# Storing the last sums of a row-sum kernel: 128 neighbouring rows, a transpose on VectorE and a last store of four pieces

## Chip, cores, metric

One core of a Trainium2 chip. The metric is the device time of one execution in microseconds (us); medians of several runs are quoted. "Issue" below is the instruction by which SyncE or ScalarE starts a transfer (a DMA), and "landing" the last of the counts on a semaphore by which the transfer tells that it is done. A "piece" is one stretch of bytes from one partition. "Tail" means the stretch from the landing of the last load to the end of the profiled span. All runs with more than one execution are fast, with a granted clock of 1.0.

## The reference

```python
batch, seq, dim = 32, 512, 1024
x = np.random.randn(batch, seq, dim).astype(np.float32)

def reference(x):
    return np.sum(x, axis=-1).astype(np.float32)
```

16,384 rows of 1024 fp32 numbers, 67.1 MB in all, each reduced to one number; the output is 64 KB.

## The kernel before

Rows are dealt out in eight groups. In each group partition p holds 16 neighbouring rows (64 KB of one piece of memory), so its 16 sums are also neighbours in the output: 64 B. Seven groups are loaded and summed mostly on VectorE; ScalarE takes half of the seventh. The eighth is cut into smaller and smaller loads (8, 5, 2 rows, then the last row in two pieces of 560 and 464 columns), so that little work is left after the last byte has landed.

```python
x_g = x.flatten_outer_dims().rearrange("(g p j) d -> g p j d", p=P, j=BIG)     # BIG = 16
out_v = out.rearrange("b s -> (b s)").rearrange("(g p j) -> p g j", p=P, j=BIG)
# ... seven groups, then of the eighth:
rows(t, 0, 8, j, 4)
rows(t, 8, 5, j + 8, 2, pairs=True)
two = rows(t, 13, 2, j + 13, 1, pairs=True)
# ...
nc.sync.dma_start(out=part, in_=rows_from(j, 1)[:, 0, :c])
nc.sync.dma_start(out=whole[:, 1 : width + 1], in_=rows_from(j, 1)[:, 0, c:])
hold(store(nc.scalar, 0, last), two, "its packets come behind those of the loads")
halves(whole[:, :1], part)               # sum of the first 560 columns
halves(sums[:, j : j + 1], whole)        # that sum and the other 464 columns
store(nc.sync, last, last + 1)           # 128 partitions, 64 B each
```

`halves` adds the two halves of a row and accumulates them in one VectorE instruction, followed by a read of the accumulator. A helper moves the wait for the last store to the instruction that clears the semaphores at the very end; all other semaphores are waited for earlier, on SyncE, ahead of two rounds of barriers.

Of the kernel before, what the change touches and what calls it, by code (L numbers as in the profile page):

```python
# [100 lines left out]
@with_exitstack  # L101
def kernel(
    ctx: ExitStack,
    tc: tile.TileContext,
    x: bass.AP,
    out: bass.AP,
):
    nc = tc.nc
    nc.at_finalize(issue_first_load_at_entry)
    nc.at_finalize(order_waits)  # L110
    nc.at_finalize(wait_for_the_store_at_the_clear)
    fp32 = mybir.dt.float32
    P = 128
    batch, seq, dim = x.shape
    rows = batch * seq
    J = rows // P
    BIG = 16


    x_g = x.flatten_outer_dims().rearrange("(g p j) d -> g p j d", p=P, j=BIG)  # L120
    out_v = out.rearrange("b s -> (b s)").rearrange("(g p j) -> p g j", p=P, j=BIG)

    def rows_from(j, n):
        return x_g[j // BIG, :, j % BIG : j % BIG + n, :]



    last = J // BIG - 1
    FIRST = 4
    pieces = (560, 464)  # L130

    with (
        tc.tile_pool(name="in", bufs=3) as inpool,
        tc.tile_pool(name="unread", bufs=4, space=bass.MemoryType.PSUM) as upool,
        tc.tile_pool(name="stage", bufs=1) as stpool,
        tc.manual_schedule(),
    ):
        sums = stpool.tile([P, J], fp32)

        def vec(dst, src):  # L140
            return nc.vector.tensor_reduce(  # L141
                out=dst, in_=src, axis=mybir.AxisListType.X, op=mybir.AluOpType.add
            )

        def hold(inst, until, reason):
            tc.add_manual_dep(
                inst.ins,
                until.ins.name,
                mybir.DependencyInfo(mybir.DependencyClass.Sync, mybir.DependencyReason.DATA),
                reason=reason,  # L150
            )

        def halves(dst, src):
            n = src.shape[-1] // 2
            return nc.vector.tensor_tensor_reduce(  # L155
                out=src[:, :n],
                in0=src[:, :n],
                in1=src[:, n:],
                scale=1.0,
                scalar=0.0,  # L160
                op0=mybir.AluOpType.add,
                op1=mybir.AluOpType.add,
                accum_out=dst,
            )

        def act(dst, src, n):
            unread = upool.tile([P, dim], fp32)
            nc.scalar.activation(  # L168
                out=unread[:, :n],
                in_=src,  # L170
                func=mybir.ActivationFunctionType.Copy,
                accum_out=dst,
            )

        sums_of = []

        def rows(t, a, n, j, n_act, pairs=False):
            nv = n - n_act
            block = t[:, a * dim : (a + n) * dim].rearrange("p (n d) -> p n d", d=dim)
            load = nc.sync.dma_start(out=block, in_=rows_from(j, n))  # L180
            if pairs:
                for q in range(nv):
                    sums_of.append(halves(sums[:, j + q : j + q + 1], block[:, q, :]))
            else:
                sums_of.append(vec(sums[:, j : j + nv], block[:, :nv, :]))
            for q in range(nv, n):
                act(sums[:, j + q : j + q + 1], block[:, q, :], dim)
            return load

        def store(eng, g0, g1):  # L190
            return eng.dma_start(
                out=out_v[:, g0:g1],
                in_=sums[:, g0 * BIG : g1 * BIG].rearrange("p (g j) -> p g j", j=BIG),
            )

        for g in range(last):
            t = inpool.tile([P, BIG * dim + 4], fp32)
            if g == 0:
                rows(t, 0, FIRST, 0, 0)
                first = sums_of[-1]  # L200
                rows(t, FIRST, BIG - FIRST, FIRST, 0)
                continue
            load = rows(t, 0, BIG, g * BIG, BIG // 2 if g == last - 1 else 0)
            if g == 1:
                hold(load, first, "no descriptors of later loads while the first ones start")

        t = inpool.tile([P, BIG * dim + 4], fp32)
        j = last * BIG
        rows(t, 0, 8, j, 4)
        rows(t, 8, 5, j + 8, 2, pairs=True)  # L210
        two = rows(t, 13, 2, j + 13, 1, pairs=True)
        a = BIG - 1



        j += a
        c, width = pieces
        whole = t[:, a * dim + c : BIG * dim + 2]
        nc.vector.memset(whole[:, width + 1 :], 0.0)  # L219
        part = t[:, a * dim : a * dim + c]  # L220
        nc.sync.dma_start(out=part, in_=rows_from(j, 1)[:, 0, :c])  # L221
        nc.sync.dma_start(out=whole[:, 1 : width + 1], in_=rows_from(j, 1)[:, 0, c:])
        hold(store(nc.scalar, 0, last), two, "its packets come behind those of the loads")
        halves(whole[:, :1], part)
        halves(sums[:, j : j + 1], whole)
        store(nc.sync, last, last + 1)


# [28 lines left out]
```

## Time and profile before

| | before |
|---|---|
| median of the first 3 runs | 162.08 us (161.59 to 162.23) |
| span of the profiled execution | 159.6 us |
| queue of loads | 97.8% of the 16 engines' span |
| VectorE, ScalarE busy | 75%, 11% |
| tail, from the last load's landing (157.43) | 2.2 us |

How to read it: an engine at 75% is not the bound where a queue of loads is at 97.8%; a change that keeps the bytes of the loads can act on the tail, or on the pace of the last loads. The lines are shown and read in the prediction. The page and its views round to 0.01 us or 0.1 us; where three decimals stand below, they are from the trace's own records of instructions, packets and semaphore counts.

### The profile page before, as it was taken

How to read it: one execution, taken by the hardware profiler on the slowest of the kernel's cores; microseconds unless marked ns; L12 is line 12 of the kernel's file. 1: busy time of each engine (PE TensorE's matmuls, PEld its weight loads, DVE VectorE, ACT ScalarE, POOL GpSimd, SP SyncE). 2: the span in 40 equal slices, each digit the busy share in tenths (PEclk: the TensorE clock that was granted, in tenths of full speed). 3: DMA queues.
4: the chain of work that ended last, by engine and by line, in shares of the span. 5: the costliest groups of instructions: out<-in, count | busy, mean ns of one | idle time of the engine just before them, and what ended most of it. 6: DMA issues, size and time to landing. Idle time of an engine off the chain costs nothing.

```text
span 159.6 us, 125 instructions
## 1 busy us (share of the span) xinstructions
DVE 120.1 (75%) x22; ACT 17.3 (11%) x31; POOL 0.2 (0%) x4
## 2 busy tenths in 40 slices
DVE  0290059960799958999499994999949999497953
ACT  3000000000000000000000000000000000496953
POOL 0000000000000000000000000000000000000000
DMA  7999996996996989979969969969969969798984
GB/s 263 460 406 579 394 526 263 526 526 263 526 526 263 526 378 411 526 312 476 526 279 509 526 263 526 526 263 526 526 263 526 509 279 526 337 452 371 467 365 128
DMA packets 2928, 67.18 MB, mean 421 GB/s; under 512 B 1264, under 2 KB 1392, under 8 KB 1520
## 3 DMA queue, kind: packets, MB, share of 16 engines
q1 hardware_dynamic: 2016, 67.12, 97.8%
q10 hardware_dynamic: 912, 0.06, 0.4%
HBM read 67.11 MB, written 0.07 MB: 421 GB/s over the span
## 4 chain that ended last, share of the span: by engine, by line
DMA 73%; DVE 25%; SPq 1%; issue 0%; DVEq 0%
DMA t<-in_x_dram 73%; DVE sums L141 24%; SPq L180 1%; SPq L221 0%; DVE t L155 0%; DVEq L252 0%
## 5 line engine op out<-in xcount | busy, mean ns | idle before, releaser
L141 DVE TENSOR_REDUCE sums<-t 128x16 f32<-128x16384 f32 (+3 forms) x9 | 116.6, 12954 | 35.3 <-DMA t<-in_x_dram 35.3
L168 ACT ACTIVATE unread<-t 128x1024 f32<-128x1024 f32 x15 | 15.2, 1012 | 139.2 <-DMA t<-in_x_dram 139.2
L155 DVE CUSTOM_DVE_ANT_0 t<-t 128x512 f32<-128x512 f32 (+2 forms) x6 | 3.5, 602 | 2.4 <-DMA t<-in_x_dram 2.4
L168 ACT ACTIVATION_READ_ACCUMULATOR unread<-t 128x1 f32 x15 | 2.8, 187 | 0.0
L168 ACT ACT_TABLE_LOAD x1 | 1.3, 1283 | 0.8 <-PEq L241 0.8
L155 DVE DVE_READ_ACCUMULATOR2_ANT sums<- 128x1 f32 x5 | 0.4, 83 | 0.0
L241 POOL MEMSET const-uint8-127<- 128x1 uint8 x1 | 0.1, 102 | 0.0
L241 POOL MEMSET const-bfloat16-1.0<- 128x1 bf16 x1 | 0.1, 101 | 0.0
L241 POOL MEMSET const-float32-0.0<- 128x1 f32 x1 | 0.1, 98 | 0.2 <-issue 0.2
L241 POOL MEMSET const-float32-1.0<- 128x1 f32 x1 | 0.1, 98 | 0.0
L155 DVE DVE_READ_ACCUMULATOR2_ANT t<- 128x1 f32 x1 | 0.1, 81 | 0.0
L219 DVE MEMSET t<- 128x1 f32 x1 | 0.1, 59 | 0.0
## 6 DMA issues: line engine op xcount, KB each, us to landing
t<-in_x_dram SPq DMA_DIRECT2D x1, 6144.0 KB, 20.9
t<-in_x_dram SPq DMA_DIRECT2D x1, 4096.0 KB, 31.1
t<-in_x_dram SPq DMA_DIRECT2D x1, 2560.0 KB, 36.9
t<-in_x_dram SPq DMA_DIRECT2D x1, 2048.0 KB, 7.1
t<-in_x_dram SPq DMA_DIRECT2D x1, 1024.0 KB, 38.9
t<-in_x_dram SPq DMA_DIRECT2D x1, 280.0 KB, 39.1
t<-in_x_dram SPq DMA_DIRECT2D x1, 232.0 KB, 39.2
t<-in_x_dram SPq DMA_DIRECT2D x6, 40.8
```

Source lines behind the costliest of these rows:

```text
L141: return nc.vector.tensor_reduce(out=dst, in_=src, axis=mybir.AxisListType.X, op=mybir.AluOpType.add)
L155: return nc.vector.tensor_tensor_reduce(out=src[:, :n], in0=src[:, :n], in1=src[:, n:], scale=1.0, scalar=0.0, op0=mybir.AluOpType.add, op ...
L168: nc.scalar.activation(out=unread[:, :n], in_=src, func=mybir.ActivationFunctionType.Copy, accum_out=dst,)
L180: load = nc.sync.dma_start(out=block, in_=rows_from(j, n))
L219: nc.vector.memset(whole[:, width + 1 :], 0.0)
L241: nc = _bacc.Bacc("TRN2", target_bir_lowering=False, num_devices=1)
```

## The change

The intent: the last store of before writes 8 KB in 128 pieces of 64 B, although only one of 16 sums in each piece is new. If the last row of each partition comes from 128 neighbouring rows, its 128 sums are 512 B in one piece of the output. VectorE turns the column of sums in blocks of 32 by 32, so that four partitions (0, 32, 64, 96) hold 32 sums each, and the last store has 4 pieces of 128 B. The other 15 sums of each partition leave earlier, by a second store on ScalarE's queue. Core of the diff:

```diff
+    SQ = 32
+    REST = BIG - 1
+    x_m = x_r[whole_groups:dense].rearrange("(p j) d -> p j d", j=REST)
+    out_m = out_r[whole_groups:dense].rearrange("(p j) -> p j", j=REST)
+    x_e = x_r[dense:]
+    out_e = out_r[dense:].rearrange("(b q) -> b q", q=SQ)
 ...
+        column = stpool.tile([P, SQ], fp32)
+        turned = stpool.tile([P, SQ], fp32)
+        nc.gpsimd.memset(column, 0.0)
 ...
-        nc.sync.dma_start(out=part, in_=rows_from(j, 1)[:, 0, :c])
-        nc.sync.dma_start(out=whole[:, 1 : width + 1], in_=rows_from(j, 1)[:, 0, c:])
-        hold(store(nc.scalar, 0, last), two, "its packets come behind those of the loads")
+        nc.sync.dma_start(out=part, in_=x_e[:, :c])
+        nc.sync.dma_start(out=whole[:, 1 : width + 1], in_=x_e[:, c:])
+        stored = nc.scalar.dma_start(
+            out=out_g, in_=sums[:, :j].rearrange("p (g j) -> p g j", j=BIG)
+        )
+        hold(stored, two, behind)
+        stored = nc.scalar.dma_start(out=out_m, in_=sums[:, j : j + REST])
+        hold(stored, two, behind)
         halves(whole[:, :1], part)
-        halves(sums[:, j : j + 1], whole)
-        store(nc.sync, last, last + 1)
+        halves(column[:, 0:1], whole)
+        nc.vector.transpose(out=turned, in_=column)
+        nc.sync.dma_start(out=out_e, in_=turned[0:P:SQ, :])
```

More of the change, by code (lines that the diff above doesn't have):

```diff
@@ L114 @@
     batch, seq, dim = x.shape
-    rows = batch * seq
-    J = rows // P
+    rows_total = batch * seq
+    J = rows_total // P
     BIG = 16
-    x_g = x.flatten_outer_dims().rearrange("(g p j) d -> g p j d", p=P, j=BIG)
-    out_v = out.rearrange("b s -> (b s)").rearrange("(g p j) -> p g j", p=P, j=BIG)
+    SQ = 32
+    REST = BIG - 1
+    last = J // BIG - 1
+    x_r = x.flatten_outer_dims()
+    out_r = out.rearrange("b s -> (b s)")
+    whole_groups = last * P * BIG
+    x_g = x_r[:whole_groups].rearrange("(g p j) d -> g p j d", p=P, j=BIG)
+    out_g = out_r[:whole_groups].rearrange("(g p j) -> p g j", p=P, j=BIG)
+    dense = rows_total - P
+    x_m = x_r[whole_groups:dense].rearrange("(p j) d -> p j d", j=REST)
+    out_m = out_r[whole_groups:dense].rearrange("(p j) -> p j", j=REST)
+    x_e = x_r[dense:]
+    out_e = out_r[dense:].rearrange("(b q) -> b q", q=SQ)
     def rows_from(j, n):
-        return x_g[j // BIG, :, j % BIG : j % BIG + n, :]
-    last = J // BIG - 1
+        g, j = divmod(j, BIG)
+        if g < last:
+            return x_g[g, :, j : j + n, :]
+        return x_m[:, j : j + n, :]
     FIRST = 4
@@ L177, in rows @@
         def rows(t, a, n, j, n_act, pairs=False):
+            sums_to = sums[:, j : j + n]
             nv = n - n_act
@@ L182, in rows @@
                 for q in range(nv):
-                    sums_of.append(halves(sums[:, j + q : j + q + 1], block[:, q, :]))
+                    sums_of.append(halves(sums_to[:, q : q + 1], block[:, q, :]))
             else:
-                sums_of.append(vec(sums[:, j : j + nv], block[:, :nv, :]))
+                sums_of.append(vec(sums_to[:, :nv], block[:, :nv, :]))
             for q in range(nv, n):
-                act(sums[:, j + q : j + q + 1], block[:, q, :], dim)
+                act(sums_to[:, q : q + 1], block[:, q, :], dim)
             return load
-        def store(eng, g0, g1):
-            return eng.dma_start(
-                out=out_v[:, g0:g1],
-                in_=sums[:, g0 * BIG : g1 * BIG].rearrange("p (g j) -> p g j", j=BIG),
-            )
         for g in range(last):
@@ L210 @@
         rows(t, 8, 5, j + 8, 2, pairs=True)
+        a = BIG - 1
         two = rows(t, 13, 2, j + 13, 1, pairs=True)
-        a = BIG - 1
-        j += a
         c, width = pieces
@@ L220 @@
         part = t[:, a * dim : a * dim + c]
-        nc.sync.dma_start(out=part, in_=rows_from(j, 1)[:, 0, :c])
-        nc.sync.dma_start(out=whole[:, 1 : width + 1], in_=rows_from(j, 1)[:, 0, c:])
-        hold(store(nc.scalar, 0, last), two, "its packets come behind those of the loads")
+        nc.sync.dma_start(out=part, in_=x_e[:, :c])
+        nc.sync.dma_start(out=whole[:, 1 : width + 1], in_=x_e[:, c:])
+        behind = "its packets come behind those of the loads"
+        stored = nc.scalar.dma_start(
[4 more added lines that the diff above has]
+        hold(stored, two, behind)
         halves(whole[:, :1], part)
-        halves(sums[:, j : j + 1], whole)
-        store(nc.sync, last, last + 1)
+        halves(column[:, 0:1], whole)
+        nc.vector.transpose(out=turned, in_=column)
+        nc.sync.dma_start(out=out_e, in_=turned[0:P:SQ, :])
 _INS = ['x']
```

## The prediction

> **What bounds the kernel now.** I read the page from the top, then the chain of waits in order of time, then the timeline of the last microseconds, because the diff touches only the last group of rows and the end. The page first: engine shares, DMA queues, totals.
>
> ```profile
> span 159.6 us, 125 instructions
> ...
> DVE 120.1 (75%) x22; ACT 17.3 (11%) x31; POOL 0.2 (0%) x4
> ...
> q1 hardware_dynamic: 2016, 67.12, 97.8%
> ...
> HBM read 67.11 MB, written 0.07 MB: 421 GB/s over the span
> ```
>
> The queue of loads keeps the 16 engines busy for 97.8% of the span, VectorE is busy for 75%: the kernel is bound by its loads. The change loads the same bytes, so it can only act after or at the very end of that stream. The chain that ended last, in order of time (start, length, what), says which work that is:
>
> ```profile
> 118.20 39.23 DMA t<-in_x_dram
> 157.43 0.02 issue
> 157.45 0.40 DVE t L155
> 157.85 0.01 DVEq L252
> ```
>
> From 118.20 it is loads without a break. The last one lands at 157.43, then one VectorE sum, and at 157.85 the body is over: 2.2 us of the 159.6 come after the stream. The timeline of those 2.2 us (start, length, engine, line, operation):
>
> ```profile
> 157.06 0.19 ACT L168 ACTIVATION_READ_ACCUMULATOR unread<-t 128x1 f32 x1
> 157.21 0.08 DVE L155 DVE_READ_ACCUMULATOR2_ANT t<- 128x1 f32 x1
> 157.45 0.40 DVE L155 CUSTOM_DVE_ANT_0 t<-t 128x233 f32<-128x233 f32 x1 [0.16 <-DMA t<-in_x_dram]
> 157.78 0.08 DVE L155 DVE_READ_ACCUMULATOR2_ANT sums<- 128x1 f32 x1
> 157.89 0.35 SPq L191 DMA_DIRECT2D out_dram<-sums  x1
> ```
>
> ScalarE has its last sum at 157.25, VectorE at 157.86, and 0.03 us later the last store (8 KB, 128 pieces of 64 B) is issued. The list of DMA issues gives the time to landing of both stores (56 KB of the first seven groups, and the last 8 KB):
>
> ```profile
> out_dram<-sums ACTq DMA_DIRECT2D x1, 56.0 KB, 2.1
> out_dram<-sums SPq DMA_DIRECT2D x1, 8.0 KB, 1.4
> ```
>
> Windows of 0.2 us (DVE, ACT, POOL busy, clock, DMA share, GB/s) cut the last store's 1.4 us into parts:
>
> ```profile
> 158.40:158.60 0.20, 0.00 (x0) 0.00 (x0) 0.00 (x0) 1.00 0.00 0
> 158.60:158.80 0.20, 0.00 (x0) 0.00 (x0) 0.00 (x0) 1.00 0.20 19
> 158.80:159.00 0.20, 0.00 (x0) 0.00 (x0) 0.00 (x0) 1.00 0.26 22
> 159.00:159.20 0.20, 0.00 (x0) 0.00 (x0) 0.00 (x0) 1.00 0.00 0
> ```
>
> The trace's packet records place the packets at 158.73 to 158.94, and its semaphore records place the 16 completion counts at 159.14 to 159.31, nearly all 0.010 us apart. So: 0.84 us from issue to first packet, 0.21 of packets, 0.37 until the last count, 1.42 in all. Then the closing instructions, by the view of line 252 (count, duration in ns, first and last start):
>
> ```profile
> L252 SPq EVENT_SEMAPHORE  x6: 17/28/28, 158.3 to 159.6; - x6
> ...
> L252 POOLq EVENT_SEMAPHORE_RANGE_CLEAR  x1: 93/93/93, 159.3 to 159.3; - x1
> ```
>
> Two paths meet at the clear, which the trace has at 159.34. One is the last store, landed at 159.31. The other is SyncE's closing waits, which begin at 158.29, once the issue is over (158.24) and the 56 KB store has landed (158.29 in the semaphore records); through two rounds of barriers they reach GpSimd at 158.98. The second path has 0.35 us of slack. From the clear to the end it is 0.29 us.
>
> **What the Trainium skill says.** (1) "DMA: Bandwidth & Descriptors", section "Why a DMA increments its semaphore by 16 and not by 1": a DMA runs on the largest count of engines up to 16 that divides the slowest dimension of both sides, and the issuer writes the rest of the 16 counts at once. The old store has 128 pieces, hence 16 engines, and the trace has 16 counts, as stated. The new one has 4 pieces, hence 4 engines; no trace of before shows that. (2) Same page, "Anatomy of one DMA": the fixed cost is about 2 us, mostly the receipt of the write. Here it is 1.42 us, of which the part after the last packet is 0.37: the fixed part dominates, but mostly ahead of the packets. (3) "VectorE: DVE Perf Modes", section "The three transpose paths": VectorE transposes 32x32 blocks only, 311 ns for 128x128 bf16. No transpose is in this trace. (4) Same DMA page, "Latency and other measured facts": row pitches of 2 MiB and up halved the rate, 512 KiB did not. Here the pitch is 64 KiB at a mean of 421 GB/s, so agreement.
>
> **The change, part by part.**
> - *Other rows for the last group.* Fifteen rows of each partition are now 60 KiB apart from the next partition's, and the last row of all partitions is one dense block of 512 KB. Piece sizes in each load stay the same (32, 20, 8 KB, then 2240 and 1856 B). The packet records of before give 91 ns for nearly every 2240 B packet and 76 to 88 for 1856 B: so even that they tell of the engine's own pace rather than of conflicts in memory. Gain of density: estimated 0, at most 0.1 us.
> - *The memset of the column* on GpSimd is at the start: 0. The last sum waits for one semaphore more, checked ahead of the load's: 0.
> - *The transpose*, on the path. Its length is an estimate: TENSOR_REDUCE takes 17,220 ns for 16,384 columns and 4,421 for 4,096, that is 1.042 ns a column and 155 fixed; 32 columns make 188 ns. From the skill's 311 ns for 128 columns, less 96 columns, 211. I take 0.20, plus 0.03 for one more hand-over (as 157.86 to 157.89 above): +0.23. Issue of the last store moves from 157.89 to 158.12.
> - *The last store in 4 pieces.* The 0.84 us ahead of the packets stays (the 56 KB store, seven times the pieces, had 0.92 there, so the count of pieces hardly matters). Packets: 0.21 falls to some 0.02. Counts: twelve fewer at 0.010 us make 0.12 less in principle, but part of that ran beside the packets; the first old count came 0.41 after the first packet, so I expect the fourth new one at 0.02 + 0.32 + 0.03. Issue to landing: 0.84 + 0.37 = 1.21, a gain of 0.21.
> - *The other 7.5 KB* go as 128 pieces of 60 B from ScalarE's queue, once ScalarE's last sum is done (157.25): issued at 157.28, landed some 1.45 us later, 158.75.
> - Sum on the store's path: 158.12 + 1.21 = 159.33 against 159.31: +0.02. On the barriers' path: the issue ends at 158.47, and there is one closing wait more (five at 0.065), so GpSimd is reached at 158.98 + 0.23 + 0.065 = 159.28, still just hidden. Span 159.65, time 162.08 + 0.02 = 162.1 us.
>
> **The rivals.**
> (a) *The barriers take over.* Their slack shrinks from 0.35 to 0.05 us. If pieces of 60 B land slowly, or if the 4-piece store lands faster than I think, SyncE's wait for the second ScalarE store sets the end: +0.1 to +0.4 us. For: the store ends only 0.05 us ahead of the waits that need it. Against: it is smaller than the 56 KB store that landed in 2.1. Chance 0.3.
> (b) *The store gains more than the transpose costs.* If the transpose is as cheap as the 1-column MEMSET (59 ns) suggests, some 0.09, and the time ahead of the packets shrinks with the number of pieces: -0.1 to -0.3 us, the barriers then being the floor. Chance 0.25.
> (c) *The dense last row loads faster.* The last 512 KB took 1.35 us (156.08 to 157.43), 388 GB/s; at 430, as the loads before them, it would be 1.22: -0.1. Against: the even packet times, which put the loss down to the short pieces. Chance 0.1.
> (d) *The new pitch slows the last loads.* They are 8 MB, some 19 us; 5% would be +1. Nothing in the profile speaks for it. Chance 0.03.
>
> **Range and chances.** Everything the change does lies within the last 2.2 us of 159.6 and nets out within some 0.3; the kernel before spread from 161.59 to 162.23 over three runs, so noise is as large as the effect. I say 162.1, and 161.6 to 162.6 for 8 in 10. A change by 2% would need 3.2 us, more than the whole tail: within 2% at 0.97, faster 0.015, slower 0.015.
>
> **What would show it.** Right: the last sum still ends 0.4 us after the last landing; a transpose of 150 to 220 ns; the store's issue 0.2 to 0.25 after the sum; issue to landing 1.2 (the list of issues); packets on the last store under 0.05 us; the clear at 159.3 to 159.4. Wrong: a transpose of over 0.3 us or under 0.1; 1.4 us to landing as before (then +0.2 overall); the ScalarE store landing after 158.8 and the clear following the barriers; a last load that lands earlier or later than 157.43 by more than 0.1.

## The result

162.12 us median (162.06 to 162.38, 4 runs) against 161.88 (161.59 to 162.23, 4 runs) for the kernel before in the same rounds. The ratio is 1.0021, 95% interval 0.9999 to 1.0043. A ratio here is the mean time of one kernel's fast runs over that of the other's of the same rounds, so it is not quite the ratio of the medians. The prediction of 162.1, within 2%, holds; by the repeat below (ratio 1.0022, interval 1.0009 to 1.0036) the change costs a little, 0.15 to 0.6 us, where the prediction had a net of 0.02.

The page of the changed kernel, the parts that answer to those of before:

```profile
span 160.3 us, 130 instructions
...
DVE 120.3 (75%) x23; ACT 17.3 (11%) x31; POOL 0.3 (0%) x5
...
q1 hardware_dynamic: 1880, 67.11, 97.4%
...
HBM read 67.11 MB, written 0.07 MB: 419 GB/s over the span
```

The same bytes, the same bound. The end of its chain in order of time (start, length, what):

```profile
118.34 39.26 DMA t<-in_x_dram
...
157.68 0.40 DVE t L174
158.09 0.02 DVE column L174
...
158.13 0.21 DVE turned L245
```

The chain has one more link, the transpose of 0.21 us. The timeline of the tail (start, length, engine, line, operation):

```profile
157.50 0.35 ACTq L241 DMA_DIRECT2D out_dram<-sums  x1
157.68 0.40 DVE L174 CUSTOM_DVE_ANT_0 t<-t 128x233 f32<-128x233 f32 x1 [0.17 <-DMA t<-in_x_dram]
158.01 0.08 DVE L174 DVE_READ_ACCUMULATOR2_ANT column<- 128x1 f32 x1
158.13 0.21 DVE L245 STREAM_TRANSPOSE turned<-column 128x32 f32<-128x32 f32 x1
158.37 0.63 SPq L246 DMA_DIRECT2D out_dram<-turned  x1
```

The last line is the surprise: the issue of a store of 4 pieces takes 0.63 us, that of 128 pieces took 0.35. The list of issues has the first two stores' time to landing (for the last one it gives none; the records of counts do):

```profile
out_dram<-sums ACTq DMA_DIRECT2D x1, 56.0 KB, 2.1
out_dram<-sums ACTq DMA_DIRECT2D x1, 7.5 KB, 1.6
out_dram<-turned SPq DMA_DIRECT2D x1, 0.5 KB
```

Windows of 0.2 us (DVE, ACT, POOL busy, clock, DMA share, GB/s) show when its packets run:

```profile
159.20:159.40 0.20, 0.00 (x0) 0.00 (x0) 0.00 (x0) 1.00 0.00 0
159.40:159.60 0.20, 0.00 (x0) 0.00 (x0) 0.00 (x0) 1.00 0.00 1
159.60:159.80 0.20, 0.00 (x0) 0.00 (x0) 0.00 (x0) 1.00 0.02 2
```

Few packets, as hoped (a share of 0.02 in one window, where before had 0.20 and 0.26 in two), but late: 1.2 us after the issue began. The closing instructions (count, duration in ns, first and last start):

```profile
L272 SPq EVENT_SEMAPHORE  x7: 17/28/28, 159.1 to 160.2; - x7
...
L272 POOLq EVENT_SEMAPHORE_RANGE_CLEAR  x1: 95/95/95, 160.0 to 160.0; - x1
```

The whole tail, from the records of both traces, in us:

| part of the tail | before | changed | difference |
|---|---|---|---|
| last load landed, to the start of the sum | 0.02 | 0.08 | +0.06 |
| sum and read of the accumulator | 0.41 | 0.41 | 0 |
| end of the sum to the issue of the last store | 0.03 | 0.27 | +0.25 |
| issue of the store to its first packet | 0.84 | 1.23 | +0.39 |
| first packet to the last completion count | 0.58 | 0.40 | -0.19 |
| landing to the end | 0.31 | 0.32 | 0 |
| sum | 2.20 | 2.71 | +0.51 |

The store gained the 0.19 us that it was meant to gain; the transpose took its 0.25; and 0.39 went to a cost that was not expected at all. So the question for the experiments: why does a store of four pieces need so long from its issue to its first packet?

### The profile page after: what moved, and what is told of

It is laid out like the page before. It is cut to its first block, busy times and chain, and to the rows that moved or that the text cites. A ratio compares the mean times of both kernels' runs of the same rounds, so it can differ in the third digit from the quotient of the medians.

```text
span 160.3 us, 130 instructions
## 1 busy us (share of the span) xinstructions
DVE 120.3 (75%) x23; ACT 17.3 (11%) x31; POOL 0.3 (0%) x5
## 3 DMA queue, kind: packets, MB, share of 16 engines
q1 hardware_dynamic: 1880, 67.11, 97.4%
## 4 chain that ended last, share of the span: by engine, by line
DMA 73%; DVE 25%; SPq 1%; issue 0%
DMA t<-in_x_dram 73%; DVE sums L160 24%; SPq L200 1%; SPq L234 0%; DVE t L174 0%; DVE turned L245 0%; DVE column L174 0%
```

## The experiments

Eleven runs. All times of ratios are against the kernel before in the same rounds. Each diff is against the changed kernel unless it says otherwise.

**1. A chain of stores.** The disputed cost by itself: behind the last store, twelve more of the same 512 B, each waiting for the landing of the one before (shortened; a memset of the last column of `sums` at the start is left out).

```diff
-        nc.sync.dma_start(out=out_e, in_=turned[0:P:SQ, :])
+        prior = nc.sync.dma_start(out=out_e, in_=turned[0:P:SQ, :])
+        for n in (4, 128, 128, 16, 16, 8, 8, 2, 2, 1, 1, 4):
+            # n == 4: turned[0:P:SQ, :]; n == 128: column[:, 0:1]; n == 1: sums[0:1, 0:P]; else sums[0 : P : P // n, 0 : P // n]
+            again = nc.sync.dma_start(out=flat.rearrange("(b q) -> b q", b=n), in_=src)
+            hold(again, prior, "one store at a time")
+            prior = again
```

> The changed kernel with twelve more stores of the same 512 B behind its last one, each waiting for the one before: 4 pieces again, then 128, 128, 16, 16, 8, 8, 2, 2, 1, 1 and 4 pieces. The longer time is of no interest; the result is right, because the last store of the chain has the right 4 pieces. Theory A (fewer than 16 engines): every store of 8, 4, 2 or 1 pieces takes about 0.63 us to issue and 1.2 us to its first packet, first and second alike; 128 and 16 pieces take 0.35 and 0.84. Rival B (first use): only the first of each kind is long, the second 4-piece store takes 0.35. Rival C (collision with the ScalarE store just ahead): only the very first store is long, all others take 0.35. Rival D (few pieces): 16 pieces are long as well.

Measured, from the records of that trace (195.11 us, one run, result right), in us:

| pieces | engines | issue | issue to landing |
|---|---|---|---|
| 4 of 128 B (the kernel's own) | 4 | 0.64 | 1.63 |
| 4 of 128 B, second and last of the chain | 4 | 0.51, 0.53 | 1.55, 1.57 |
| 128 of 4 B, adjacent in memory | 16 | 0.34, 0.34 | 7.96, 9.89 |
| 16 of 32 B | 16 | 0.54, 0.51 | 1.71, 1.66 |
| 8 of 64 B | 8 | 0.61, 0.60 | 1.63, 1.62 |
| 2 of 256 B | 2 | 0.49, 0.47 | 1.49, 1.46 |
| 1 of 512 B | 1 | 0.27, 0.24 | 1.09, 1.08 |

Theory A falls: 16 pieces on 16 engines are as slow to issue as 4 on 4, and one piece on one engine is the fastest of all. Rival B and C fall in their strong form, for the second 4-piece store, issued in quiet, still takes 0.51. Few pieces as such (D) are not it either, since one piece is fast. What sets the slow rows apart is that their partitions lie apart (every 8th, 16th, 32nd, 64th); that became theory S. And the 4 B pieces showed something that nobody had asked: they issue fast and take 8 to 10 us to land.

**2. The transpose left out.**

```diff
-        nc.vector.transpose(out=turned, in_=column)
-        nc.sync.dma_start(out=out_e, in_=turned[0:P:SQ, :])
+        nc.sync.dma_start(out=out_r[dense:].rearrange("(p o) -> p o", o=1), in_=column[:, 0:1])
```

> The changed kernel without the transpose: the 128 sums of the dense last row go out as 128 pieces of 4 B straight from the column, on 16 engines; the row layout and the second ScalarE store stay. Theory A: the issue takes 0.35 us as before, 0.84 to the first packet, 1.42 to landing, and the issue comes 0.03 after the sum; so the time falls back to that of the kernel before, ratio to it 0.999 to 1.001, and against the changed kernel -0.45 us after the last load's landing. Rival C (the second ScalarE store's packets, just ahead, slow the SyncE store): issue still about 0.6 and the time stays 0.2 to 0.4 us above before. A rival that blames the row layout for the loss would also leave the last load's landing 0.2 us late.

168.15 us median (5 runs), ratio 1.0393 (1.0372 to 1.0414): a miss by 6 us. The issue was 0.35 us, as expected, with the second ScalarE store in place, so rival C falls again. But the landing is not 1.4 (list of issues of this run, KB and us to landing):

```profile
out_dram<-column SPq DMA_DIRECT2D x1, 0.5 KB, 7.6
```

In the dense layout the transpose is thus worth some 6 us, 168.15 against 162.07 of the changed kernel in the same rounds. The trace's packet records end 1.04 us after the issue, as those of the kernel before do (1.05): what takes long comes after them. The transpose repairs a damage that the dense layout itself does; the kernel before, whose pieces are 64 B, never had it.

**3. Sixteen pieces on sixteen engines, with the transpose.** The last 128 outputs are wrong.

```diff
-        nc.sync.dma_start(out=out_e, in_=turned[0:P:SQ, :])
+        nc.sync.dma_start(
+            out=out_r[dense:].rearrange("(b q) -> b q", q=8), in_=turned[0:P:8, 0:8]
+        )
```

> The changed kernel with the transpose kept, but the last store takes 16 pieces of 32 B from 16 partitions, hence 16 engines; the last 128 outputs are wrong on purpose. Theory A: issue 0.35 us, first packet at 0.84, landing about 1.33 after the issue; the transpose's 0.24 remains, so about 0.29 us faster than the changed kernel and 0.15 us slower than the kernel before (ratio to before 1.001). Rival D (few pieces): issue 0.6 and the time as that of the changed kernel, ratio 1.002.

162.39 us median, ratio 1.0044 (1.0024 to 1.0064), no faster than the changed kernel. The timeline has the issue:

```profile
158.58 0.55 SPq L246 DMA_DIRECT2D out_dram<-turned  x1
```

Landing came 1.69 us after the issue. The number of engines is not the cause in the kernel either.

**4. The changed kernel again**, no edit.

> The changed kernel once more, beside the two others on one chip: 162.1 to 162.4, ratio to before 1.002 to 1.003 by both theories; its trace tells whether the issue of 0.63 us and the last load's landing 0.18 us later than in the trace of before come again. If the late landing is chance, it moves by that much here.

162.07 us median (161.97 to 162.30, 5 runs), ratio 1.0022 (1.0009 to 1.0036). The issue was again 0.63 us, the landing 1.61 after it, the tail 2.70. The last load landed at 157.81.

**5. A chain of shapes.** A chain like the first, of 25 stores whose shapes separate step, number and width, and three more with the right outputs (the diff is shortened).

```diff
+        for n in (128, 64, 32, 16, 8, 4, 2, 1):
+            pieces_of(n, 1, 16)              # 64 B from n neighbouring partitions
+        for n in (64, 32, 16, 8, 4, 2):
+            pieces_of(n, P // n, 16)         # 64 B from n partitions that lie apart
+        for step in (1, 32, 1, 32):
+            pieces_of(4, step, 32)           # 4 x 128 B
+        for width in (16, 8, 4, 2, 1):
+            pieces_of(P, 1, width)           # 128 adjacent pieces, 64 B down to 4 B
+        for apart in (16, 128):
+            ...                              # 128 x 4 B, 64 B and 512 B apart in memory
```

> The first chain threw out the count of engines: 16 pieces on 16 engines took 0.51 to 0.54 us to issue, 128 pieces 0.34, one piece 0.25. Here a longer chain of stores behind the last one, one at a time: pieces of 64 B from 128, 64, 32, 16, 8, 4, 2 and 1 neighbouring partitions; pieces of 64 B from 64, 32, 16, 8, 4 and 2 partitions that lie apart (step 2 to 64); 128 B from 4 partitions, neighbouring and 32 apart, twice; 128 adjacent pieces of 64, 32, 16, 8 and 4 B; 128 pieces of 4 B that are 64 B and 512 B apart; then the right outputs once more, so the result is right. Theory S (step): stores from neighbouring partitions issue in 0.35 or less, those from partitions apart in 0.5 to 0.65. Theory N (number): 2 to 64 partitions are slow whatever the step. For the 4 B pieces, theory L (several pieces in one 64 B of memory are written one after another): the landing grows as the pieces get smaller, 1.4 at 64 B, some 2 to 4 at 16 and 8 B, 8 to 10 at 4 B adjacent, and falls to about 1.4 when the 4 B pieces are 64 B apart. Rival Z (small pieces are slow in themselves): 4 B pieces take 8 to 10 us however far apart.

The two forms of 4 pieces of 128 B, in the timeline of that run (neighbouring partitions first, then 32 apart):

```profile
180.81 0.26 SPq L252 DMA_DIRECT2D out_dram<-sums  x1
...
181.94 0.54 SPq L252 DMA_DIRECT2D out_dram<-sums  x1
```

The same bytes, pieces, engines and destination; only the step between the partitions differs. From the records, in us (issue / issue to landing):

| partitions, 64 B each | neighbouring | apart |
|---|---|---|
| 128 | 0.34 / 1.41 | |
| 64 | 0.52 / 1.70 | 0.50 / 1.69 |
| 32 | 0.35 / 1.34 | 0.49 / 1.65 |
| 16 | 0.32 / 1.34 | 0.52 / 1.66 |
| 8 | 0.28 / 1.16 | 0.62 / 1.67 |
| 4 | 0.25 / 1.11 | 0.53 / 1.56 |
| 2 | 0.24 / 1.04 | 0.49 / 1.48 |
| 1 | 0.23 / 1.03 | |
| 4, of 128 B, twice | 0.26 / 1.12, 1.11 | 0.54, 0.52 / 1.57, 1.57 |

Theory S holds in these shapes, with one exception that stays unexplained: 64 neighbouring partitions are slow as well. What makes the step costly is not shown, and step and reach were not separated: every store with a step also reached over at least half of the 128 partitions. Theory N fails. Of the 128 adjacent pieces, 64 B landed in 1.42 us, 32 B in 1.46, 16 B in 2.03, 8 B in 3.23 and 4 B in 7.25. The same 4 B pieces 64 B or 512 B apart landed in 1.40. So it is not their smallness (rival Z fails): small pieces that lie next to each other cost, as theory L says. That 64 B is the unit is not shown: no distance between 4 B and 64 B was tried, and 32 B pieces, two to 64 B, cost only 0.04 us. Nor does the chain show how they are handled there; the packet records of all these stores end 1.02 to 1.05 us after the issue.

**6. The kernel before again**, no edit to it.

> The kernel before, submitted as if it were a change: ratio 0.999 to 1.001. Its trace shows whether the last load's landing at 157.43 in the first trace is chance: four traces of the changed rows had it at 157.57 to 157.81. If the row layout delays the loads, this one is again near 157.4 to 157.5; if it is chance, it may be anywhere from 157.4 to 157.8. Issue of the last store again 0.35 us, landing 1.42.

161.75 us median, ratio 1.0003 (0.9984 to 1.0022). Its timeline:

```profile
157.78 0.08 DVE L155 DVE_READ_ACCUMULATOR2_ANT t<- 128x1 f32 x1
158.01 0.40 DVE L155 CUSTOM_DVE_ANT_0 t<-t 128x233 f32<-128x233 f32 x1
158.33 0.08 DVE L155 DVE_READ_ACCUMULATOR2_ANT sums<- 128x1 f32 x1
158.44 0.35 SPq L191 DMA_DIRECT2D out_dram<-sums  x1
```

The last load landed at 157.96 here, later than in the first trace of before (157.43) and later than in most traces of the changed rows (157.51 to 157.81 in eight of the ten beside the first, 158.28 and 158.50 in the other two). So the landing that was 0.18 us later in the first trace of the changed kernel is within chance, and no effect of the row layout on the loads is shown. The tail is 2.22 us, as before.

**7. One store of the same form early on.**

```diff
                 hold(load, first, "no descriptors of later loads while the first ones start")
+                nc.sync.dma_start(out=out_e, in_=column[0:P:SQ, :])
```

> The changed kernel with one more 4-piece store of the same form from the same queue, early in the kernel (its zeros are overwritten at the end). In the chain the first 4-piece store took 0.64 us to issue and later ones 0.51 and 0.53. Rival B (first use) in its weak form: the last store's issue falls to 0.51 to 0.54, the time by 0.1 us against the changed kernel. If it is the long idle time of the queue that costs the 0.1, nothing changes: 0.63 and ratio to before 1.002.

The issue fell:

```profile
158.53 0.54 SPq L247 DMA_DIRECT2D out_dram<-turned  x1
```

So some 0.1 us of the 0.63 goes with the first use of that form (one trace), and the tail is 2.63 in place of 2.70. The time does not show it: 162.24, ratio 1.0039 (1.0018 to 1.0060). The rest of the excess over 0.26 is there on every use.

**8. The second ScalarE store left out** (wrong).

```diff
-        stored = nc.scalar.dma_start(out=out_m, in_=sums[:, j : j + REST])
-        hold(stored, two, behind)
```

> The changed kernel without the second ScalarE store (15 of 16 outputs of the last group stay unwritten, wrong on purpose). Rival C (its descriptors or packets delay the SyncE store): the last store's issue falls from 0.63 to about 0.5 and the first packet comes earlier. Otherwise issue 0.63, landing 1.62, and the time as the changed kernel's within 0.1 us, for the closing waits have some slack.

The issue stays:

```profile
158.28 0.62 SPq L244 DMA_DIRECT2D out_dram<-turned  x1
```

Landing 1.62 us after it, tail 2.70, ratio 1.0030 (1.0005 to 1.0055). Rival C, the collision, is out for good.

**9. Four neighbouring partitions in the kernel itself** (96 outputs wrong: only partition 0 holds what belongs there).

```diff
-        nc.sync.dma_start(out=out_e, in_=turned[0:P:SQ, :])
+        nc.sync.dma_start(out=out_e, in_=turned[0 : P // SQ, :])
```

> The changed kernel, but the last store reads partitions 0 to 3 in place of 0, 32, 64 and 96: the same 4 pieces of 128 B on 4 engines, wrong values in 96 outputs on purpose. Theory S (partitions that lie apart make the issue slow): issue 0.26 to 0.35 us in place of 0.63, landing 1.1 to 1.2 after the issue in place of 1.63. Then the store lands ahead of the closing barriers, which start from the second ScalarE store's landing (about 1.5 us after the last load's) and need 0.6 more, so the end is set by them: about 2.4 us from the last load's landing to the end in place of 2.7, against 2.2 in the kernel before. Ratio to before 1.001; against the changed kernel -0.3 us. If the step is not it: 2.7 and ratio 1.002 to 1.003.

The store did as theory S says (timeline), and landed 1.16 us after its issue, at 160.43:

```profile
159.26 0.35 SPq L246 DMA_DIRECT2D out_dram<-turned  x1
```

The time, however, did not fall: 162.13, ratio 1.0035 (1.0013 to 1.0057), and the tail of the traced run, which was the slowest of its six (162.96), is 2.67. In that trace the end is set by the other path; the other five runs have no trace. The list of issues has the second ScalarE store:

```profile
out_dram<-sums ACTq DMA_DIRECT2D x1, 7.5 KB, 1.9
```

Issued at 158.39, it landed at 160.29. By its list of waits SyncE waits 0.4 us for it, in its closing waits, and goes on at 160.31 (in the changed kernel it did not wait for it); the barriers take until 160.81, and the clear follows at 160.89, 0.46 us after the last store has landed. In the other traces this store took 1.44 to 1.85 us, so 1.9 is an extreme; with the changed kernel's own 1.58 the tail would be some 2.4, an estimate. The expected 2.4 and ratio 1.001 were missed in this run; the rival of the prediction that the barriers take over is seen at work.

**10. Four transposes into one partition row.** The only correct kernel of these that avoids partitions apart: one piece of 512 B.

```diff
-        nc.vector.transpose(out=turned, in_=column)
-        nc.sync.dma_start(out=out_e, in_=turned[0:P:SQ, :])
+        row = stpool.tile([SQ, P], fp32)
+        for q in range(0, P, SQ):
+            nc.vector.transpose(out=row[:, q : q + SQ], in_=column[q : q + SQ, :])
+        nc.sync.dma_start(out=out_r[dense:].rearrange("(o b) -> o b", o=1), in_=row[0:1, :])
```

> The changed kernel with four transposes of one block each in place of one of four blocks, all into the same 32 partitions, so that the 128 sums lie in one partition and the last store is one piece of 512 B; the result is right. In the first chain such a store took 0.25 us to issue and 1.08 to land. Theory S: landing 1.1 after the issue. The four transposes are not measured yet: one of four blocks took 0.21; if each of the four takes that in turn it is 0.84 in all, if they overlap some 0.5. So from the sum's end to landing 1.6 to 2.0 us, against 1.9 in the changed kernel and 1.45 in the kernel before: between 0.3 us faster and 0.1 slower than the changed kernel, ratio to before 1.001 to 1.003. To beat the kernel before, the four would have to take under 0.3 us.

162.31 us, ratio 1.0047 (1.0029 to 1.0064), result right. Timeline:

```profile
158.12 0.84 DVE L247 STREAM_TRANSPOSE row<-column 32x32 f32<-32x32 f32 x4
158.99 0.32 SPq L248 DMA_DIRECT2D out_dram<-row  x1
```

The store landed 1.11 us after its issue, as expected, but the four transposes run strictly one behind another, 0.21 us apart, and cost 0.63 more than one. The ratio is above the expected 1.001 to 1.003, and it beats neither kernel. Here too the closing barriers set the end: the store landed at 160.09, they reached GpSimd at 160.11, and the clear followed at 160.19.

**11. Both obstacles away:** neighbouring partitions and no second ScalarE store (wrong twice over; the edits of 8 and 9 together).

> Both obstacles taken away at once: the last store reads partitions 0 to 3 (issue 0.35, landing 1.16 in the run before) and the second ScalarE store is left out, so that the closing barriers no longer wait for it (wrong on purpose twice over). If the two ends account for the whole loss, the end is set by the last store again: from the last load's landing 0.08 to the sum, 0.41 for it, 0.25 for the transpose and its hand-overs, 1.16 to landing, 0.32 to the end, together 2.2 us as in the kernel before; ratio to before 0.999 to 1.001. If something else costs time (the rows of the last group), the tail is 2.2 all the same, but the ratio stays at 1.002 or more.

161.56 us median, ratio 1.0002 (0.9981 to 1.0023). The issue is short:

```profile
158.28 0.35 SPq L244 DMA_DIRECT2D out_dram<-turned  x1
```

Landing came 1.16 us after it, and the tail is 2.28. With both taken away the changed kernel stands, within the noise, where the kernel before stands, transpose included; the interval still overlaps that of the changed kernel (1.0009 to 1.0036), so it is the tail of the trace, 2.28 against 2.70, that shows the gain. The end was not quite set by the store, as expected: it landed at 159.44, GpSimd was reached at 159.42, and the clear, 0.08 us behind the barriers as in experiments 9 and 10, began at 159.50. Behind the landing alone it began 0.02 after it (the kernel before and the changed one), so the barriers cost 0.04.

No correct version that beats both kernels came out of this. It would need the 128 sums in neighbouring partitions for under about 0.3 us of VectorE time (an estimate: 1.45 us from the sum's end to landing in the kernel before, less 1.11 to 1.16 for such a store), with barriers that come no later than in the kernel before; and the transpose of blocks leaves the sums 32 apart.

## Why the prediction was right, and where it was not

The time, the range and "within 2%" held. That 162.1 was hit so closely is luck: the three runs that it started from had a median of 162.08, while those of the kernel before in the later rounds had 161.55 to 161.78. That high start made up for the 0.34 us by which the net was too small. By its own steps:

- *Bound by loads, change in the tail only.* Right: 97.4% after, same bytes, and experiment 6 shows no difference in the loads that exceeds chance.
- *Other rows for the last group: gain 0.* Not contradicted. The packets of the dense row took a flat 76 and 91 ns in the first trace (before: 76 to 88 and 91 to 104, where the prediction's "nearly every" 2240 B packet at 91 ns was 87 of 128). But the repeats turn this round: before again has 91 for all 128 and 76 for 112 of 128, the changed kernel again 76 to 88 and 91 to 98. So the evenness is no effect of the rows, and no gain in the landing is shown.
- *The last sum's extra semaphore: 0.* Off by a few hundredths. The wait ahead of the load's took 0.050 us in place of 0.021, and from the load's landing to the sum it was 0.08 us against 0.02 and 0.05 in the two traces of before. VectorE comes to that wait only after the sum of the first piece. In all eleven traces of the changed rows the sum started 0.13 us after that wait had begun, wherever the load's landing lay (0.07 to 0.11 us ahead of the sum), so there the wait set the start, and it is not as free as the prediction took it.
- *The transpose: +0.23.* Right: 0.211 us long, +0.25 with its hand-overs.
- *Packets and counts: a gain of 0.21.* Right: 0.19, though the packets took 0.08 us, not 0.02 or "under 0.05".
- **"The 0.84 us ahead of the packets stays … the count of pieces hardly matters."** This step failed. It measured 1.23, so the landing came 1.63 us after the issue in place of 1.21; with four neighbouring partitions in the same kernel it was 0.77 (experiment 9). The number of pieces indeed matters little among neighbouring partitions (1.03 to 1.41 us to landing for 1 to 128 of them, apart from 64), but the prediction had looked only at stores from 128 neighbouring partitions and did not ask what a step of 32 partitions does: 0.26 against 0.54 us of issue, 0.73 against 1.18 to the first packet, and 1.11 against 1.57 to landing, in the same chain. Why a step costs this is open. Some 0.1 of the kernel's own 1.63 is that of a first use.
- *The second ScalarE store: landed by 158.75.* Late by 0.33 (its own sum, 157.28 + 1.45, makes 158.73). Of this 0.22 is a later issue (157.50), behind a last sum on ScalarE that ended 0.22 later in this trace. The rest is the store itself: it took 1.58 us, and 1.44 to 1.90 in other runs. Alone in the second chain, from SyncE's queue, the same pieces took 1.42. What delays it in the kernel was not looked into.
- *The barriers stay just hidden.* Right: GpSimd was reached at 159.91, the store landed at 159.99. But where the barriers came last (experiments 9 to 11) the clear began 0.08 us after they had reached GpSimd, so only 0.03 us were to spare in place of 0.05, and the slack in the kernel before was 0.28, not 0.35. They stayed hidden only because the slower store moved its own landing back; rival (a) appears as soon as the store is fast (experiments 9 to 11). One reading was wrong without harm: SyncE's closing waits did not begin with the 56 KB store's landing at 158.29. In both traces of the kernel before they begin 0.05 us after the issue ends, and the wait for that store is the third of them. Rivals (b), (c) and (d) did not come about.

The net of 0.02 us was thus mis-sized mainly by one term, +0.39 ahead of the packets, and by 0.06 ahead of the sum; the measured tails differ by 0.51 us and the times by 0.36 (1.0022 of 161.75, with the interval from 0.15 to 0.58). The prediction was right in the total because either sum is small beside the noise of single runs; its mechanism was right but for the stretch from issue to first packet, the wait ahead of the sum and the reading of the closing waits.

## What to carry to other kernels

Count not only the pieces of a small store but look at where they start: four pieces from partitions 32 apart took 0.46 us longer to land than four from neighbouring ones, more than going from 128 pieces to 4 could save. A layout that makes the output of the last step dense in memory can leave many tiny pieces next to each other, which was worth 6 us here; the 64 B pieces of the old layout had no such trouble. When a tail is shortened, look at which other wait stands just behind the one removed: here it was the closing barriers, 0.03 us away.

## What the Trainium skill lacked or had wrong

- "DMA: Bandwidth & Descriptors" has no word on how the issue of a store from SyncE depends on the step between its source partitions: 0.26 us (neighbouring) against 0.54 (32 apart) for 4 x 128 B, 1.11 against 1.57 to landing. Nor on 64 neighbouring partitions, which took 0.52 and 1.70.
- Same page, "Specifications", says that transfers under 512 B are read and written back, without telling that neighbours matter: 128 pieces of 4 B took 7.3 to 9.9 us adjacent and 1.40 when 64 B apart; 16 B pieces took 2.03, 32 B pieces 1.46.
- Same page, "Why a DMA increments its semaphore by 16 and not by 1", says that the issuer writes the missing counts at once, without waiting for data, and gives no time. The changed kernel's trace has five updates for the 4-piece store, as the rule of the page for the number of engines has it. The first of them, which comes ahead of any packet and so should be the issuer's, came 1.01 us after the issue began (0.48 with neighbouring partitions), 0.38 after it ended.
- Same page, "Anatomy of one DMA", gives a fixed cost of some 2 us for transfers issued from GpSimd; no such sum stands there for stores from SyncE. Those of 64 B to 8 KB took 1.03 to 1.70 us here, one at a time and in pieces of 64 B or more.
- "VectorE: DVE Perf Modes", "The three transpose paths", has no fp32 figure: 128x32 took 0.211 us, as one of the prediction's two estimates had it (the page's 311 ns for 128x128 bf16, less 96 columns at the 1.042 ns of the trace); transposes of one block took 0.20 each, 0.21 from start to start.
